# Weight splits moved to the front of the planner's order, and part of the state-space tables moved from GpSimd to VectorE and ScalarE

## The chip, the cores and the metric

The kernel runs on one core of a Trainium2 chip. The metric is the device time of one launch in microseconds (us); the median of the runs is what is compared. The profile comes from an execution of its own, and times in it are counted from the first instruction. PE is TensorE, DVE is VectorE, ACT is ScalarE, POOL is GpSimd, SP is the engine whose queue issues most of the transfers.

## The reference, cut to what matters

Two layers work on a residual stream x of 256 tokens by 2048 features, all in float32.

```
layer 0: h = rmsnorm(x);  [q k v u z_a z_b] = h @ w_in        # 2048 -> 6144
         o_a = chunked_attention(q, k, v) * silu(z_a)          # 16 heads x 64
         y   = gelu(s5(u));  o_b = y * sigmoid(y @ w_glu + b) * silu(z_b)
         x   = x + [o_a o_b] @ w_out
layer 1: h = rmsnorm(x);  [q k v z f] = h @ w_in               # forgetting attention, 16 heads x 128
         x   = x + (attention * silu(z)) @ w_out
out    = rmsnorm(x)
```

`s5` is a state-space model: for each of 64 groups of 16 channels, a state of 64 complex numbers follows x_t = A x_(t-1) + B u_t, with y_t = Re(C x_t) + D u_t. A, B and C are computed from small parameters; this is where the tables of this kernel come from.

## The kernel before, in words

**The weight stream.** Every large product is cut into column tiles of 512. For each, `project` (L135) walks over the K dimension in chunks of two 128-row blocks; `next_w` (L116) fetches a chunk (128 x 1024 float32, 512 KB) through SP's queue into `wr` (four buffers) and splits it into a rounded high part `wh` (L131, on ACT) and the rest `wl` (L132, on DVE), three buffers each. PE then does, for both blocks and both token tiles, three matmuls (high by high, L142; low weight, L143; low activation, L144), so 12 matmuls per chunk. A chunk's `wh` buffer comes free when PE has done its last matmul. There are 292 such whole chunks: a few in front for `u`, then z_b (first half), z_a, q, k, v in halves, z_b (second half), the GLU, the output projection `oe`, the 16 projections of layer 1 (`cq`, `ck`, `cv`, `cz` for four groups of heads) and its output projection `oo`.

**The state-space model.** It is done in blocks of 8 time steps. After the first half of `u` is projected, DVE computes powers of A for all groups (`pr`, `pi`, `psg`, L254 to L312). `tables(e)` then runs for e = 0..7, eight slots of groups each. It loads `bc`, and makes on DVE `bb`, `bw` (six instructions of 128 x 128, L331 to L336) and `w1` (three of 128 x 1024, L350 to L352). On POOL it makes `cc` (two of 128 x 128, L337 and L338) and `mx` (three of 128 x 1152, L357 to L359). `w1` is transposed on PE (`pm`, L366) into `min`; `mx` is stored to memory (`m_d`, L360) and multiplied with `bb` on PE (`pk`, L374) into kernels `ks`, stored as `k_d`. With the transposed input `uT`, PE forms `pv` (L408), DVE and ACT copy it (`vs`, L411 to L413), PE transposes it (`pvt`, L417) and ACT writes `X` (L419). When all eight are in, DVE runs a serial scan over the blocks: 30 steps of four instructions of 128 x 128 (L428 to L431). `s5_final` (L498) reads `k_d` and `m_d` back (L503, L508), multiplies on PE (`py`, L514 and L518), applies gelu (L520) and transposes into `yTh`, `yTl` (L536, L537), the input of the GLU product `acc_glu`.

**What can go on without the scan.** The projections z_b, z_a, q, k, v of layer 0 need only the normalised input. The GLU product needs `yTh` and `yTl`.

**What sets the order.** Tile's planner (`schedule_with_timeline_sim=True`) simulates the program and gives every engine a fixed order: among the instructions that are ready at a simulated moment, the one written earliest goes first. On the chip each engine then executes its own list strictly in that order, with semaphores between engines. `tables(0)` to `tables(2)` are written ahead of the second `u` tile, the others ahead of the gates, so table work and the scan are ahead, in priority, of the splits for z_b, z_a, q, k and v. The transfers of the weights keep their place on SP's queue.

Of the kernel before, what the change touches and what calls it, by code (L numbers as in the profile page):

```python
# [9 lines left out]
F32 = mybir.dt.float32  # L10
F32R = mybir.dt.float32r
AF = mybir.ActivationFunctionType
ALU = mybir.AluOpType
# [4 lines left out]
P = 128  # L18
L = 256
D = 2048  # L20
NT = 512
CK = 2
# [13 lines left out]
LN2_2 = math.log(2.0) - LN2_1  # L36
MAGIC = 12582912.0
PI_F = 3.1415925


@with_exitstack
def trunk(ctx: ExitStack, tc: tile.TileContext, a, out: bass.AP):
# [22 lines left out]
    nc.gpsimd.memset(mhalf, -0.5)  # L65

    def rstd_of(parts, name, n=2):
        """(sum of parts / D + EPS) ** -0.5 for n token tiles"""
        ms, r, c = (const.tile([P, n], F32, name=f"{w}_{name}") for w in ("ms", "rs", "rc"))
        nc.vector.tensor_reduce(ms, parts, axis=AX.X, op=ALU.add)  # L70
        nc.vector.tensor_scalar(ms, ms, 1.0 / D, EPS, op0=ALU.mult, op1=ALU.add)
        nc.gpsimd.tensor_tensor(r, ms, mhalf[:, 0:n], op=ALU.pow)
        nc.vector.tensor_tensor(c, r, r, op=ALU.mult)
        nc.vector.tensor_tensor(c, c, ms, op=ALU.mult)
        nc.vector.tensor_scalar(c, c, -0.5, 1.5, op0=ALU.mult, op1=ALU.add)
        nc.vector.tensor_tensor(r, r, c, op=ALU.mult)
        return r

    def vexp(pool, dst, src, n, key):
        """dst = exp(src) on [P, n], to float32's accuracy: 2^k times a polynomial"""  # L80
        V = nc.vector
        xc, kf, r, p_ = (pool.tile([P, n], F32, name=f"ve{i}_{key}", tag=f"ve{i}", bufs=1) for i in range(4))
        ki = pool.tile([P, n], mybir.dt.int32, name=f"vei_{key}", tag="vei", bufs=1)
        V.tensor_scalar(xc, src, 89.0, -90.0, op0=ALU.min, op1=ALU.max)
        V.tensor_scalar(kf, xc, 1.0 / math.log(2.0), MAGIC, op0=ALU.mult, op1=ALU.add)
        V.tensor_scalar(kf, kf, MAGIC, -127.0, op0=ALU.subtract, op1=ALU.max)
        V.scalar_tensor_tensor(r, kf, -LN2_1, xc, op0=ALU.mult, op1=ALU.add)
        V.scalar_tensor_tensor(r, kf, -LN2_2, r, op0=ALU.mult, op1=ALU.add)
        V.tensor_scalar(kf, kf, 127.0, None, op0=ALU.add)
        V.tensor_copy(ki, kf)  # L90
        V.tensor_scalar(ki, ki, 23, None, op0=ALU.logical_shift_left)
        V.tensor_scalar(p_, r, 1.0 / 5040.0, None, op0=ALU.mult)
        for c in (1.0 / 720.0, 1.0 / 120.0, 1.0 / 24.0, 1.0 / 6.0, 0.5, 1.0):
            V.scalar_tensor_tensor(p_, p_, c, r, op0=ALU.add, op1=ALU.mult)
        V.scalar_tensor_tensor(dst, p_, 1.0, ki.bitcast(F32), op0=ALU.add, op1=ALU.mult)

    def split_T(src, c, g, dh, dl, name):
        """transpose 4 K-blocks (columns c*512..) of both token tiles, scaled by g,
        into the feature-major hi/lo pair"""
        for half in range(2):  # L100
            pt = ps_tr.tile([P, 2, L], F32, name=f"pt_{name}_{c}_{half}", tag="tr")
            for kk in range(2):
                kb = c * 4 + half * 2 + kk
                for t in range(2):
                    nc.tensor.transpose(pt[:, kk, t * P:(t + 1) * P],
                                        src[:, t, kb * P:(kb + 1) * P], ident)
            for kk in range(2):
                kb = c * 4 + half * 2 + kk
                nc.scalar.activation(dh[:, kb, :], pt[:, kk, :], AF.Copy, scale=g[:, kb:kb + 1])
                nc.vector.scalar_tensor_tensor(dl[:, kb, :], pt[:, kk, :], g[:, kb:kb + 1],  # L110
                                               dh[:, kb, :].bitcast(F32), op0=ALU.mult, op1=ALU.subtract)

# [1 line left out]
    wpos = [0]  # L114

    def next_w(split=None, dst=None):  # L116
        i = wpos[0]
        wpos[0] += 1
        raw = wp.tile([P, CK * NT], F32, name=f"wr_{i}", tag="wr", bufs=4)
        if dst:  # L120
            wh, wl = dst
        else:
            wh = wp.tile([P, CK * NT], F32R, name=f"wh_{i}", tag="wh", bufs=3)
            wl = wp.tile([P, CK * NT], F32R, name=f"wl_{i}", tag="wl", bufs=3)
        step = NT if split else CK * NT
        for o in range(0, CK * NT, step):
            c = slice(o, o + step)
            nc.sync.dma_start(raw[:, c], a["w"][i][:, c])
            if split:
                split(o // NT)  # L130
            nc.scalar.activation(wh[:, c], raw[:, c], AF.Copy)  # L131
            nc.vector.tensor_tensor(wl[:, c], raw[:, c], wh[:, c].bitcast(F32), op=ALU.subtract)  # L132
        return wh, wl

    def project(ah, al, nkb, name, ready=None, by_token=False):  # L135
        """one 512-column tile of the next product for both token tiles"""
        acc = [ps_acc.tile([P, NT], F32, name=f"acc_{name}_{t}", tag="acc") for t in range(2)]

        def block(kb, wh, wl, t):
            c = slice(kb % CK * NT, (kb % CK + 1) * NT)  # L140
            sh, sl = ah[:, kb, t * P:(t + 1) * P], al[:, kb, t * P:(t + 1) * P]
            nc.tensor.matmul(acc[t], sh, wh[:, c], start=kb == 0, stop=False)  # L142
            nc.tensor.matmul(acc[t], sh, wl[:, c], start=False, stop=False)  # L143
            nc.tensor.matmul(acc[t], sl, wh[:, c], start=False, stop=kb == nkb - 1)  # L144

        if by_token:
            for t in range(2):
                for kb in range(nkb):
                    block(kb, *ready[kb // CK], t)
        else:  # L150
            for kc in range(nkb // CK):
                wh, wl = ready[kc] if ready else next_w()
                for kb in range(kc * CK, (kc + 1) * CK):
                    for t in range(2):
                        block(kb, wh, wl, t)
        return acc

    # ================= layer 0 =================
    xTh = actp.tile([P, 16, L], F32R, name="xTh", tag="ah")
    xTl = actp.tile([P, 16, L], F32R, name="xTl", tag="al")  # L160
    l0 = ctx.enter_context(ExitStack())
# [39 lines left out]
    k_d = dram.tile([NGQ, P, 2 * TC * GC], F32, name="k_d")  # L201
    m_d = dram.tile([8, P, 8, TC * GC], F32, name="m_d")

    # u columns
    uts = []
    for n in range(2):
        if n == 1:
# [16 lines left out]
                nc.scalar.activation(ut, acc[t], AF.Copy, scale=r0[:, t:t + 1])  # L224
                nc.sync.dma_start(u_d[t * P:(t + 1) * P, NT:], ut)
        if n == 0:
# [1 line left out]
            def sm(name):  # L228
                return s5.tile([P, G], F32, name=name, tag="sm_" + name)

# [84 lines left out]
            def tables(e):  # L315
# [18 lines left out]
                V.tensor_tensor(bw, bc[:, :, 1, :], gb(cr), op=ALU.mult)  # L334
                V.tensor_tensor(tt, bc[:, :, 0, :], gb(ncs), op=ALU.mult)
                V.tensor_tensor(bw, bw, tt, op=ALU.add)  # L336
                W.tensor_scalar(cc[:, 0], bc[:, :, 2, :], nsgn, None, op0=ALU.mult)  # L337
                W.tensor_scalar(cc[:, 1], bc[:, :, 3, :], -1.0, None, op0=ALU.mult)  # L338

                def pw(t_, sl):  # L340
                    n_ = len(range(9)[sl])
# [12 lines left out]
                mx = s5.tile([P, 8, 9, GC], F32, name=f"mx_{e}", tag="mx", bufs=2)  # L354
                tm = s5.tile([P, 8, 9, GC], F32, name=f"tm_{e}", tag="tm", bufs=1)
                fwd = slice(0, 9)
                W.tensor_tensor(mx, pw(pr, fwd), cc[:, 0].unsqueeze(2).to_broadcast([P, 8, 9, GC]), op=ALU.mult)  # L357
                W.tensor_tensor(tm, pw(pi, fwd), cc[:, 1].unsqueeze(2).to_broadcast([P, 8, 9, GC]), op=ALU.mult)
                W.tensor_tensor(mx, mx, tm, op=ALU.add)  # L359
                nc.sync.dma_start(m_d[e], mx[:, :, 1:9, :].rearrange("p s l c -> p s (l c)"))  # L360

                mi_ = s5b.tile([P, 8, P], F32, name=f"min_{e}", tag="min", bufs=4)
# [68 lines left out]
        V.tensor_tensor(X[:, :, :, n + 1], st1, st2, op=ALU.add)  # L431


    # gates
    zb = l0p.tile([P, 2, 2 * NT], F32, name="zb")
    zaT = l0p.tile([P, 8, L], F32, name="zaT")
    def gate(z_, nm, n):
# [16 lines left out]
    yTh = at.tile([P, 8, L], F32R, name="yTh", bufs=1)  # L454
    yTl = at.tile([P, 8, L], F32R, name="yTl", bufs=1)
    def scores(qT, kT, rows, keys):
        """causal score blocks of the heads that lie in the given rows, one row tile beside the other"""
        pscs = [ps_sc.tile([P, 3, P], F32, name=f"psc_{key}", tag="sc") for key in keys]
        for psc, r in zip(pscs, rows):
            nc.tensor.matmul(psc[:, 0, :], qT[r, 0:P], kT[r, 0:P], start=True, stop=True)  # L460
# [2 lines left out]
        return pscs  # L463

    def probs(pool, psc, bias0, bias1, key, scaled=False):
        """softmax numerators of one head, transposed per key block, and 1/sum"""
        lg = pool.tile([P, 3, P], F32, name=f"lg_{key}", tag="lg")
        mx_ = pool.tile([P, 2], F32, name=f"mx_{key}", tag="mxs", bufs=3)
        nc.vector.tensor_tensor_reduce(lg[:, 0, :], psc[:, 0, :], bias0, 1.0, LOWEST,
# [18 lines left out]
        return pT, rs  # L488

    def out_T(o_, w, dh, dl, kb, key):  # L490
        """o_ [P, 2, 128] token-major -> hi/lo K-block"""
        po = ps_tr.tile([P, L], F32, name=f"po_{key}", tag="tr")
        for t in range(2):
            nc.tensor.transpose(po[:, t * P:(t + 1) * P], o_[:, t, :], ident)
# [99 lines left out]

    gate(zb, "zb", 1)

    # GLU
    for n in range(2):
        c = slice(n * NT, (n + 1) * NT)
        y = catx.tile([P, 2, NT], F32, name=f"y_{n}")  # L600
# [25 lines left out]
        split_T(x, n, gO, x1Th, x1Tl, "x1")  # L626
    l0.close()

    # ================= layer 1 =================
    l1 = ctx.enter_context(tc.tile_pool(name="l1", bufs=2))  # L630
    r1 = rstd_of(ssp1, "1")
    r1q = const.tile([P, 2], F32, name="r1q")
# [2 lines left out]
    oTl = l1.tile([P, 16, L], F32R, name="oTl", bufs=1)  # L635

    def forget():
        # forget gates
        tri = l1.tile([P, 3 * P], F32, name="tri", bufs=1)
        nc.gpsimd.memset(tri[:, 0:P], 0.0)  # L640
        nc.gpsimd.memset(tri[:, P:3 * P], 1.0)
# [121 lines left out]
    for n in range(3):  # L763
        acc = project(oTh, oTl, 16, f"oo{n}")
        for t in range(2):
            xs = add_tile(n, acc, t)
            nc.gpsimd.tensor_tensor(xs, xs, gF[:, n * NT:(n + 1) * NT], op=ALU.mult)
    # the last tile goes one token tile after the other, its weights held on chip
    lh = actp.tile([P, 4, CK * NT], F32R, name="lh", tag="ah")
    ll = actp.tile([P, 4, CK * NT], F32R, name="ll", tag="al")  # L770
    lx = [l1.tile([P, CK * NT], F32R, name=f"lx{i}", tag="cqk") for i in range(2)]
# [13 lines left out]
            nc.sync.dma_start(ov[:, t, c * NT:(c + 1) * NT], xs)  # L785


# [1 line left out]
def _lay(inputs):  # L789
    import numpy as np  # L790

    f = {k: np.asarray(v) for k, v in inputs.items()}

    def tiles(w, n0, n1):
        """[K, N] -> chunks [(n1-n0) * K/(CK*128), 128, CK*512] of the column tiles n0..n1"""
        w = w[:, n0 * NT:n1 * NT]
        K, N = w.shape
        w = w.reshape(K // (CK * P), CK, P, N // NT, NT).transpose(3, 0, 2, 1, 4)
# [64 lines left out]
```

## Time and profile before

| what | value |
|---|---|
| runs (us) | 997.0, 997.74, 1001.69; median 997.74 |
| profiled execution, span of its instructions | 995.2 us; the page lists no other time for that execution |
| busy: PE, DVE, ACT, POOL | 946.9, 626.4, 495.7, 184.6 us |
| transfers | 191.47 MB, mean 192 GB/s |
| PE's share of the chain that ended last | 74%; DVE 15% |

The span is the time from the first to the last instruction, and the median of the runs is 2.5 us above it. A row of the page's groups gives a line, an engine, output and inputs with their shapes, a count, the busy time and the mean of one instruction in ns, and last how long the engine had been idle before these instructions and who released it. PEclk is the clock that TensorE was granted, 1.00 being full speed. Neighbouring instructions of an engine overlap by about 0.1 us in the records.

### The profile page before, as it was taken

The page shows a single profiled execution, that of the slowest core. Times are in us where ns is not written, and L with a number is a line of the kernel's source. Part 1 is how long each engine was busy: PE and PEld are TensorE (multiplying, and loading weights), DVE is VectorE, ACT ScalarE, POOL GpSimd, SP SyncE. Part 2 cuts the span into 40 slices and gives each one's busy share as a digit, 9 for nine tenths or more (in the row PEclk, how much of TensorE's full clock was granted, in tenths as well). Part 3 has the DMA queues.
Part 4 walks back from the last instruction along what each step waited for, and adds up shares of the span by engine and source line. Part 5 has one row for each costly group of instructions (what it writes and reads, how often), then busy time and mean ns, then how long its engine had stood idle before and what let it go on. Part 6 is the DMA issues. An engine that isn't in the chain of part 4 may idle for free.

```text
span 995.2 us, 13310 instructions
## 1 busy us (share of the span) xinstructions
PE 946.9 (95%) x4828; PEld 762.9 (77%) x4828; DVE 626.4 (63%) x1071; ACT 495.7 (50%) x717; POOL 184.6 (19%) x182
## 2 busy tenths in 40 slices
PE   7968788999999999999999999999999999999996
PEld 5856566887776777788888888888888888888874
DVE  7899999499962467855555445444544554455464
ACT  6623444454463367654444555445645554555451
POOL 2297974100003011000000321011001100100210
PEclk9987999999999999999999999999999999999998
DMA  8774655875569965566664654555455545554652
GB/s 303 281 218 147 189 165 175 241 214 178 163 204 263 266 207 179 167 200 204 204 225 149 212 195 153 190 182 191 155 191 184 170 153 191 185 170 155 194 196 90
DMA packets 72577, 191.47 MB, mean 192 GB/s; under 512 B 7488, under 2 KB 27184, under 8 KB 72128
## 3 DMA queue, kind: packets, MB, share of 16 engines
q1 hardware_dynamic: 71520, 188.93, 59.5%
q0 software_dynamic: 992, 1.69, 0.9%
q8 instruction: 38, 0.62, 0.3%
q14 instruction: 27, 0.22, 0.1%
HBM read 180.09 MB, written 10.50 MB: 192 GB/s over the span
## 4 chain that ended last, share of the span: by engine, by line
PE 74%; DVE 15%; DMA 4%; issue 4%; SPq 1%; ACT 1%; POOL 0%; POOLq 0%; DVEq 0%; ACTq 0%
DVE wl L132 5%; PE acc_oe L143 3%; PE acc_oe L142 3%; PE acc_oe L144 3%; PE acc_cv L142 3%; PE acc_cq L143 3%; PE acc_cq L144 3%; PE acc_cq L142 3%; PE acc_ck L142 3%; PE acc_cv L144 3%; PE acc_cv L143 3%; PE acc_cz L143 3%; PE acc_cz L144 3%; PE acc_cz L142 3%; PE acc_ck L144 3%
## 5 line engine op out<-in xcount | busy, mean ns | idle before, releaser
L132 DVE TENSOR_TENSOR wl<-wr,wh 128x1024 fp32r<-128x1024 f32 (+1 forms) x292 | 372.9, 1280 | 281.5 <-ACT wh L131 278.6
L131 ACT ACTIVATE wh<-wr 128x1024 fp32r<-128x1024 f32 (+1 forms) x292 | 307.6, 1056 | 338.8 <-PE acc_ck L144 41.8
L722 POOL TENSOR_SCALAR cbt<-ckb,cum 128x128 f32<-128x128 f32 x16 | 17.8, 1111 | 323.7 <-DVE mx_c L471 265.4
L143 PE MATMUL acc_cv<-wl,x1Th 128*128 128x512 f32 x128 | 51.1, 399 | 0.0
L143 PE MATMUL acc_oe<-wl,cTh 128*128 128x512 f32 x128 | 51.0, 399 | 0.0
L143 PE MATMUL acc_cq<-wl,x1Th 128*128 128x512 f32 x128 | 50.8, 397 | 0.0
L143 PE MATMUL acc_cz<-wl,x1Th 128*128 128x512 f32 x128 | 50.6, 395 | 0.0
L144 PE MATMUL acc_cq<-wh,x1Tl 128*128 128x512 f32 x128 | 50.5, 395 | 0.0
L144 PE MATMUL acc_oe<-wh,cTl 128*128 128x512 f32 x128 | 50.5, 395 | 0.0
L144 PE MATMUL acc_cv<-wh,x1Tl 128*128 128x512 f32 x128 | 50.3, 393 | 0.0
L144 PE MATMUL acc_cz<-wh,x1Tl 128*128 128x512 f32 x128 | 50.2, 392 | 0.0
L143 PE MATMUL acc_ck<-wl,x1Th 128*128 128x512 f32 x128 | 49.9, 390 | 0.0
L144 PE MATMUL acc_ck<-wh,x1Tl 128*128 128x512 f32 x128 | 49.9, 390 | 0.0
L142 PE MATMUL acc_cq<-wh,x1Th 128*128 128x512 f32 x128 | 48.7, 400 | 0.0
L142 PE MATMUL acc_cz<-wh,x1Th 128*128 128x512 f32 x128 | 47.6, 400 | 0.0
L142 PE MATMUL acc_oe<-wh,cTh 128*128 128x512 f32 x128 | 47.6, 399 | 0.0
L142 PE MATMUL acc_cv<-wh,x1Th 128*128 128x512 f32 x128 | 47.3, 398 | 0.0
L142 PE MATMUL acc_ck<-wh,x1Th 128*128 128x512 f32 x128 | 46.5, 392 | 0.0
L143 PE MATMUL acc_oo<-wl,oTh 128*128 128x512 f32 x108 | 42.5, 393 | 0.5 <-DVE wl L132 0.5
L144 PE MATMUL acc_oo<-wh,oTl 128*128 128x512 f32 x108 | 42.2, 391 | 0.0
L142 PE MATMUL acc_oo<-wh,oTh 128*128 128x512 f32 x108 | 39.7, 394 | 0.0
L143 PE MATMUL acc_zb<-wl,xTh 128*128 128x512 f32 x64 | 28.3, 442 | 9.4 <-DVE wl L132 9.4
(391 smaller groups left out, 2137.9 us busy)
## 6 DMA issues: line engine op xcount, KB each, us to landing
wr<-in_w_dram SPq DMA_DIRECT2D x295, 512.0 KB, 3.5
m_d<-mx SPq DMA_DIRECT2D x8, 512.0 KB, 4.9
mo<-m_d SPq DMA_DIRECT2D x8, 512.0 KB, 7.5
T<-k_d SPq DMA_DIRECT2D x40, 64.0 KB, 6.7
bc<-in_s5bc_dram SPq DMA_DIRECT2D x8, 256.0 KB, 3.3
xt<-in_x_dram SPq DMA_DIRECT2D x2, 1024.0 KB, 8.2
k_d<-ks SPq DMA_DIRECT2D x8, 256.0 KB, 3.4
bt<-in_rbx_dram SPq DMA_DIRECT2D x8, 256.0 KB, 3.7
```

The costliest lines, as they stand in the source:

```text
L131: nc.scalar.activation(wh[:, c], raw[:, c], AF.Copy)
L132: nc.vector.tensor_tensor(wl[:, c], raw[:, c], wh[:, c].bitcast(F32), op=ALU.subtract)
L142: nc.tensor.matmul(acc[t], sh, wh[:, c], start=kb == 0, stop=False)
L143: nc.tensor.matmul(acc[t], sh, wl[:, c], start=False, stop=False)
L144: nc.tensor.matmul(acc[t], sl, wh[:, c], start=False, stop=kb == nkb - 1)
L722: W.tensor_scalar(bt[:, 0, :], ckb[:, hh, 0:P], cum[:, 0, h:h + 1], None, op0=ALU.add)
```

## The change

Two edits. In `next_w` the two split instructions are traced inside a block that lets the planner treat them as though they had been written 3000 instructions earlier; the fetch stays as it was. In `tables(e)` the two `cc` instructions go from POOL to ACT, and the three `mx`/`tm` instructions go from POOL to DVE; what POOL keeps there are two memsets. Comments and docstrings are dropped too. Two extra lines move the numbering: L131, L132 become L133, L134, and so on.

```diff
+SPLIT_AHEAD = 3000
...
             if split:
                 split(o // NT)
-            nc.scalar.activation(wh[:, c], raw[:, c], AF.Copy)
-            nc.vector.tensor_tensor(wl[:, c], raw[:, c], wh[:, c].bitcast(F32), op=ALU.subtract)
+            with tc.high_priority(offset=SPLIT_AHEAD):
+                nc.scalar.activation(wh[:, c], raw[:, c], AF.Copy)
+                nc.vector.tensor_tensor(wl[:, c], raw[:, c], wh[:, c].bitcast(F32), op=ALU.subtract)
...
-                W.tensor_scalar(cc[:, 0], bc[:, :, 2, :], nsgn, None, op0=ALU.mult)
-                W.tensor_scalar(cc[:, 1], bc[:, :, 3, :], -1.0, None, op0=ALU.mult)
+                nc.scalar.activation(cc[:, 0], bc[:, :, 2, :], AF.Copy, scale=nsgn)
+                nc.scalar.activation(cc[:, 1], bc[:, :, 3, :], AF.Copy, scale=-1.0)
...
-                W.tensor_tensor(mx, pw(pr, fwd), cc[:, 0].unsqueeze(2).to_broadcast([P, 8, 9, GC]), op=ALU.mult)
-                W.tensor_tensor(tm, pw(pi, fwd), cc[:, 1].unsqueeze(2).to_broadcast([P, 8, 9, GC]), op=ALU.mult)
-                W.tensor_tensor(mx, mx, tm, op=ALU.add)
+                V.tensor_tensor(mx, pw(pr, fwd), cc[:, 0].unsqueeze(2).to_broadcast([P, 8, 9, GC]), op=ALU.mult)
+                V.tensor_tensor(tm, pw(pi, fwd), cc[:, 1].unsqueeze(2).to_broadcast([P, 8, 9, GC]), op=ALU.mult)
+                V.tensor_tensor(mx, mx, tm, op=ALU.add)
```

## The prediction, made before the changed kernel was run

> **What bounds the kernel now.** I read the busy times by stage first, with stretches cut where the work changes: the tables (50 to 180 us), the scan (200 to 275), the end of the state-space model (296 to 350), then layer 0's rest and layer 1.
>
> ```profile
> core 0: us, PE busy (x) PEld busy (x) DVE busy (x) ACT busy (x) POOL busy (x), PEclk, DMA share, GB/s
> 0.00:50.00 50.00, 42.93 (x176) 34.58 (x177) 39.78 (x129) 32.54 (x45) 13.43 (x23) 1.00 0.82 292
> 50.00:180.00 130.00, 104.81 (x615) 80.11 (x614) 125.47 (x125) 52.30 (x81) 96.62 (x48) 0.89 0.60 183
> 180.00:200.00 20.00, 20.00 (x135) 16.00 (x134) 8.34 (x11) 9.44 (x14) 3.97 (x9) 1.00 0.87 230
> 200.00:275.00 75.00, 72.21 (x341) 57.37 (x340) 73.33 (x180) 37.62 (x57) 0.53 (x2) 1.00 0.60 187
> 296.00:350.00 54.00, 50.77 (x451) 37.26 (x451) 20.03 (x25) 20.25 (x28) 9.60 (x19) 0.97 1.02 262
> 420.00:950.00 530.00, 530.00 (x2506) 438.28 (x2505) 270.97 (x414) 270.25 (x366) 49.13 (x72) 1.00 0.56 184
> 950.00:995.20 45.20, 35.13 (x153) 28.15 (x151) 22.70 (x33) 14.71 (x21) 5.08 (x4) 0.92 0.42 140
> ```
>
> PE bounds nearly everything: from 420 to 950 us it is busy all the time at full clock, so nothing there can be won. The place that is open is 50 to 180: PE works 104.81 of 130 us at clock 0.89, while DVE is busy 125.47. At full clock its work is 104.81 x 0.89 = 93.3 us, so 130 - 93.3 = **36.7 us** are lost there: 25.2 idle, 11.5 by the clock. The 7 us before the first matmuls and the 10 us at the end are untouched by the edits. Next, what PE waits for in that stretch, and what one such wait looks like in order of time:
>
> ```profile
> PE acc_za L143 <- DVE wl L132: 9.6, 5, 4.1
> PE acc_zb L143 <- DVE wl L132: 9.4, 4, 5.7
> PE pm L366 <- DVE w L352: 3.7, 2, 2.2
> PE pvt L417 <- DVE vs L413: 1.4, 1, 1.4
> PE pv L408 <- DVE ks L380: 1.1, 1, 1.1
> ```
> ```profile
> 70.71 3.71 POOL L359 TENSOR_TENSOR mx<-mx,tm 128x1152 f32<-128x1152 f32 x1
> 71.84 3.66 DVE L352 TENSOR_TENSOR w<-w,tw 128x1024 f32<-128x1024 f32 x1
> 72.31 0.40 PE L144 MATMUL acc_zb<-wh,xTl 128*128 128x512 f32 x1
> 72.54 0.40 PE L143 MATMUL acc_zb<-wl,xTh 128*128 128x512 f32 x1
> 75.56 1.28 PE L366 MATMUL pm<-ident,w 128*128 128x128 f32 x8 [2.16 <-DVE w L352]
> 77.06 0.63 PE L144 MATMUL acc_zb<-wh,xTl 128*128 128x512 f32 x1
> 77.48 0.63 PE L142 MATMUL acc_zb<-wh,xTh 128*128 128x512 f32 x1
> ```
>
> 19.0 of the 25.2 idle us wait for `wl`, always DVE; 6.2 wait for results of the tables. And DVE is slow for a reason: its `w` starts at 71.84, POOL's `mx` ends at 74.42, and `w` ends at 75.50, 1.1 us after that. It stood still until POOL was done. After the wait, matmuls start 0.42 us apart (77.06, 77.48) where just before it was 0.23 (72.31, 72.54).
>
> **What leaves POOL, and what its instructions cost DVE.** The groups of POOL and DVE, those of DVE in the table stretch, the last two DVE rows and the split in the scan stretch serving as its undisturbed price:
>
> ```profile
> L359 POOL TENSOR_TENSOR mx<-mx,tm 128x1152 f32<-128x1152 f32 x8 | 27.1, 3385 | 0.4
> L357 POOL TENSOR_TENSOR mx<-pr,cc 128x1152 f32<-128x1152 f32 x8 | 25.2, 3154 | 7.0 <-DVE rs L76 4.6 <-DMA m_d<-mx 2.4
> L358 POOL TENSOR_TENSOR tm<-pi,cc 128x1152 f32<-128x1152 f32 x8 | 21.4, 2675 | 0.7 <-DVE pi L287 0.7
> L337 POOL TENSOR_SCALAR cc<-bc,nsgn 128x128 f32<-128x128 f32 x8 | 16.1, 2015 | 20.8 <-DVE ve_dt L88 16.5 <-DMA bc<-in_s5bc_dram 4.3
> L327 POOL MEMSET bb<- 128x256 f32 x8 | 2.6, 325 | 4.8 <-PE pk L374 4.8
> ```
> ```profile
> L132 DVE TENSOR_TENSOR wl<-wr,wh 128x1024 fp32r<-128x1024 f32 x27 | 47.7, 1778 | 0.9 <-ACT wh L131 0.9
> L352 DVE TENSOR_TENSOR w<-w,tw 128x1024 f32<-128x1024 f32 x8 | 18.1, 2260 | 0.1
> L351 DVE TENSOR_TENSOR tw<-psg,bw 128x1024 f32<-128x1024 f32 x8 | 10.0, 1247 | 0.1
> L333 DVE TENSOR_TENSOR bb<-bb,tt 128x128 f32<-128x128 f32 x8 | 9.0, 1130 | 0.0
> L336 DVE TENSOR_TENSOR bw<-bw,tt 128x128 f32<-128x128 f32 x8 | 6.8, 846 | 0.1
> L334 DVE TENSOR_TENSOR bw<-bc,cr 128x128 f32<-128x128 f32 x6 | 5.8, 962 | 0.6 <-DMA bc<-in_s5bc_dram 0.6
> L332 DVE TENSOR_TENSOR tt<-bc,cs 128x128 f32<-128x128 f32 x8 | 2.5, 316 | 0.0
> ```
> ```profile
> L132 DVE TENSOR_TENSOR wl<-wr,wh 128x1024 fp32r<-128x1024 f32 x24 | 29.2, 1222 | 1.5 <-ACT wh L131 1.5
> L431 DVE TENSOR_TENSOR X<-st,st 128x128 f32<-128x128 f32 x30 | 12.1, 402 | 0.8
> ```
>
> The same split takes 1.778 us here and 1.222 in the scan, where POOL is busy 0.53 of 75 us. The excess: splits 27 x 0.556 = 15.0; `w` 8 x (2.260 - 1.222) = 8.3; against the 0.316 of L332, L333 8 x 0.814 = 6.5, L336 8 x 0.530 = 4.2, L334 6 x 0.646 = 3.9. That is 37.9 us of DVE time that is waiting, not work. All of it goes with POOL's operations, since only memsets of about 0.3 us stay.
>
> The Trainium skill says the same in SBUF — State Buffer, "Who interferes with whom": a VectorE instruction with two SBUF inputs and a GpSimd instruction that reads SBUF exclude each other for the whole instruction, while GpSimd writing alone does not. By that rule the memsets left on POOL cost nothing and every two-input row above may be held. The `w` row that ends 1.1 us after `mx` agrees.
>
> **What DVE gains in work.** 24 instructions of 128 x 1152. No row shows them on DVE; the nearest is L351, which reads the same power table in the same broadcast form: 1.247 for 1024, so 1.40 for 1152, 24 x 1.40 = **33.7 us**. From below, the split's 1.222 as it stands gives 29; from above, POOL's own prices give 27.1 + 25.2 + 21.4 = 73.7. I take 33.7, since L351 is of the same engine and form. DVE in the stretch then needs 125.5 - 37.9 + 33.7 = 121.3 (about 117 to 161 by the ends): almost no relief of its load by itself. The gain must come from the order.
>
> **What ACT gains.** 16 copies of 128 x 128 with a scale. The nearest is a larger copy:
>
> ```profile
> L411 ACT COPY vs<-pv 128x256 f32<-128x256 f32 x8 | 3.0, 373 | 3.2 <-PE pv L408 3.2
> ```
>
> At most 16 x 0.373 = 6 us, against 77 us in which ACT is idle from 50 to 180; from below, nothing. On the path of a table it replaces POOL's 2.0 us. It is taken as nothing; without that cover it is 6.
>
> **The order.** A split is now taken as soon as its chunk and its buffer are there, ahead of tables, scan and attention. One chunk feeds PE for 12 x 0.23 = 2.7 us and asks 1.2 of DVE and about as much of ACT. So PE can be fed always, and DVE's other half is left to the tables. What is pushed back: `bb`, `w`, `mx`, and behind them `pm`, `pk`, `pv`, the scan, `s5_final`. Let the tables be done T after 50. DVE's share without splits is 121.3 - 27 x 1.222 = 88; the splits take 1.222 / 2.73 = 0.45 of the time PE gives to chunks. Of PE's 93.3, 324 chunk matmuls at 0.23 make 74, so 19 go to small ones. T = 88 + 0.45 (T - 19), T = 144: the tables end at 194 rather than 180. In these 144 us PE does 144 of work where it now does 93 + 14 = 107 (the 14 from the busy row 180 to 200). So PE is the full **36.7 us** further, and the tables are 14 late. Who waits for them:
>
> ```profile
> L431 DVE TENSOR_TENSOR X<-st,st x30: 386/403/417, 202.5 to 271.0; 128x128 f32<-128x128 f32 x30
> L518 PE MATMUL py<-mo,X x128: 272/273/421, 296.2 to 337.0; 128*32 128x128 f32 x128
> L537 DVE TENSOR_TENSOR yTl<-pyt,yTh x4: 680/686/692, 344.0 to 350.1; 128x512 fp32r<-128x512 f32 x4
> L142 PE MATMUL acc_glu<-wh,yTh x32: 388/389/499, 376.4 to 404.4; 128*128 128x512 f32 x32
> ```
>
> The scan ends at 271.4, `py` starts 25 us later although nothing more is computed for it, `yTl` is done at 350.8 and the GLU starts at 376. Slack of 25 and 25, 50 together. Needed are 14 (later tables) + 36.7 (PE arriving earlier) = 51. So the slack is just eaten up: I charge 3 us.
>
> **What stays lost.** The scan stretch shows what DVE at 73.33 of 75 leaves idle on PE without POOL: 2.8 us. Over 130 us that is 4.8. Of the 6.2 us for table results, which the splits' rank doesn't cure, half was POOL's holding; 3 stay. Together 8 (from 0 to 15 with some slow clock behind each gap).
>
> **Sum.** 995.2 - 36.7 + 8 + 3 = 969.5 for the span; the median of the runs lies 997.74 - 995.2 = 2.5 above it: **972 us**.
>
> **Rivals.**
>
> 1. *The tables become the bound* (20%). If the moved instructions cost 1.75 us rather than 1.40, DVE has 8.4 more, the tables end 8.4 / 0.55 = 15 later, and the GLU waits for that beyond the 3 charged: 972 + 12 = 984. At about 2.05 us each the gain would be gone. For it: slack is used up to a microsecond. Against: L351.
> 2. *No clock loss, nothing late* (10%). All gaps that stay are short, so the clock holds at 1.00, and the 2.8 us of the scan stretch close too: 995.2 - 36.7 - 2.8 + 5 + 2.5 = 963. For it: 1.00 in the scan stretch, whose gaps are short. Against: 77.06, slow after gaps of no more than 2.16 us. TensorE: Matmul & The Clock Gate, "What's actually happening", in the Trainium skill has the clock fall after an idle window of about 3.4 us; by that rule this result would be likelier, and the row after 2.16 us doesn't agree.
> 3. *The rank does nothing* (10%): splits wait for buffers that PE frees, not for their turn. Then DVE's 121.3 for 125.5 stays, and the gain is 4 plus half of the clock loss: 995.2 - 10 + 2.5 = 988. Against: 5.7 us of wait in one piece, longer than any buffer turn of 2.7.
> 4. *Slower: a split at the head of DVE's queue stands waiting for `wh`, and tables and scan stand behind it* (9%). The work to the scan's end is 88 + 4 x 30 x 0.40 = 136 us of DVE. With w us of standing per chunk its share is 1 - (1.222 + w) / 2.73. After the scan 55 us follow at least (296 to 351, first `py` to last `yTl`). For a GLU start at 376, as now, the scan must end at 321, in 271 us: share 0.502, w = 0.14. Past that point the change loses; at w = 0.25 the share is 0.46, the scan ends at 345, the GLU starts at 400: 24 us late, 995.2 + 24 + 2.5 = 1022. For it: in-order queues, and w enters each of 80 chunks. Against: the scan row shows 1.5 us of such idle for 24 splits, 0.06 each.
>
> The forecast has 51%, its own range 962 to 982. A difference of 0.5% (5 us) is about what a measurement of this kernel can tell from none. Under 992.7 lie the forecast and rivals 1, 2 and 3, less a twentieth for the upper part of 1 and 3: faster 0.85, same 0.06, slower 0.09. The range takes in rival 2 and most of 1 and 3: 957 to 990.
>
> **What would show it.** Right: split and table rows of DVE at 1.22 and 0.3 in the table stretch, the moved rows near 1.4, POOL nearly idle there, PE over 95% busy at clock 0.97 or more, PE's waits for `wl` under 5 us. The step on slack: the GLU starting near 340 with no wait of PE between the scan's end and it; a wait for `py` or `yTh` there of over 10 us is rival 1. Wrong: DVE idle before splits in the table stretch (rival 4), moved rows at 2 us or more, or table rows still held with POOL idle. Layer 1 should be as long as before; a gap there would be something that I haven't seen.

## The result and the profile after

The changed kernel takes 974.81 us (971.64 to 975.55, median of four) against 997.39 us before: a ratio of 0.9762, interval 0.9736 to 0.9787. The forecast was 972. The time was met; the experiments below show that the edit on which most of the gain was put, the rank of the splits, brought none of it.

Busy time by stretch of the changed kernel, the columns as in the prediction:

```profile
50.00:180.00 130.00, 124.33 (x791) 98.88 (x790) 115.05 (x163) 67.27 (x110) 7.68 (x21) 0.97 0.77 241
180.00:200.00 20.00, 20.00 (x100) 16.54 (x98) 18.48 (x41) 11.54 (x16) 0.00 (x0) 1.00 0.62 175
200.00:275.00 75.00, 70.93 (x384) 53.48 (x383) 66.22 (x177) 37.14 (x66) 1.32 (x5) 1.00 0.54 172
275.00:296.00 21.00, 17.83 (x138) 13.67 (x136) 7.35 (x6) 8.29 (x10) 5.78 (x12) 0.99 1.06 246
296.00:350.00 54.00, 52.13 (x343) 39.39 (x344) 25.77 (x45) 23.10 (x38) 5.74 (x8) 0.91 0.84 236
420.00:950.00 530.00, 530.00 (x2501) 438.17 (x2500) 275.31 (x413) 265.78 (x360) 50.65 (x74) 1.00 0.56 185
```

Counted as in the prediction (stretch less PE's busy time at the granted clock), the table stretch now loses 130 - 124.33 x 0.97 = 9.4 us where it lost 36.7: 27.3 us won. Part is given back later. The stretch 200 to 275 loses 4.1 (2.8 before), and what lies between 275 and 350 loses 3.4 + 6.6 = 10.0 (4.8 before, all of it from 296 on). In layer 1 nothing moved: 530.00 of 530.00, as before.

VectorE's groups in the table stretch, and ScalarE's two new ones:

```profile
L134 DVE TENSOR_TENSOR wl<-wr,wh 128x1024 fp32r<-128x1024 f32 x36 | 43.6, 1217 | 3.0 <-ACT wh L133 2.9
L360 DVE TENSOR_TENSOR tm<-pi,cc 128x1152 f32<-128x1152 f32 x8 | 10.8, 1349 | 0.3 <-ACT cc L340 0.3
L354 DVE TENSOR_TENSOR w<-w,tw 128x1024 f32<-128x1024 f32 x8 | 9.7, 1215 | 0.0
L335 DVE TENSOR_TENSOR bb<-bb,tt 128x128 f32<-128x128 f32 x8 | 2.2, 280 | 0.0
```
```profile
L339 ACT ACTIVATE cc<-bc,nsgn 128x128 f32<-128x128 f32 x6 | 2.4, 400 | 5.4 <-DMA bc<-in_s5bc_dram 5.4
L340 ACT ACTIVATE cc<-bc 128x128 f32<-128x128 f32 x6 | 1.8, 294 | 0.0
```

Each VectorE row that was held before is at its undisturbed price again: the split 1.217 us (1.778 before), `w` 1.215 (2.260), `bb` 0.280 (1.130). Nine more splits fit into the same 130 us, beside the work that came from GpSimd. What PE still waits for in the first 420 us, the five longest behind the start (at the start it waits 6.3 us for the first `wh`, as before):

```profile
PE py L520 <- DMA mo<-m_d: 3.3, 3, 2.1
PE acc_zb L145 <- DVE wl L134: 2.3, 1, 2.3
PE pm L368 <- DVE w L354: 1.9, 1, 1.9
PE py L516 <- DMA T<-k_d: 1.6, 1, 1.6
PE acc_q L145 <- DVE wl L134: 1.6, 3, 0.7
```

The waits of `acc_za` and `acc_zb` for a split, 19.0 us between 50 and 180 us before, are 2.3 now. The longest in total, behind the start, is now for the read-back of `m_d`. The state-space chain, the store of the tables before and after, then scan, `yTl` and GLU after:

```profile
L360 SPq DMA_DIRECT2D m_d<-mx x8: 524/525/608, 68.8 to 170.6; - x8
```
```profile
L362 SPq DMA_DIRECT2D m_d<-mx x8: 524/525/597, 66.7 to 161.0; - x8
L433 DVE TENSOR_TENSOR X<-st,st x30: 377/398/414, 182.2 to 253.6; 128x128 f32<-128x128 f32 x30
L539 DVE TENSOR_TENSOR yTl<-pyt,yTh x4: 680/686/692, 324.0 to 329.9; 128x512 fp32r<-128x512 f32 x4
L144 PE MATMUL acc_glu<-wh,yTh x32: 389/389/500, 353.4 to 381.0; 128*128 128x512 f32 x32
```

The last table is stored 10 us earlier, the scan ends 17 us earlier (254.0 for 271.4), and the GLU starts 23 us earlier (353.4 for 376.4). The whole gain is there by that point, and the tables didn't fall behind for it: VectorE's last `w` ends at 170.9 us, where it ended at 172.5.

### The profile page after: what moved, and what is told of

It reads as the page before. It is cut to its first block, busy times and chain, and to the rows that moved or that the text cites. A ratio compares the mean times of both kernels' runs of the same rounds, so it can differ in the third digit from the quotient of the medians.

```text
span 973.5 us, 13313 instructions
## 1 busy us (share of the span) xinstructions
PE 941.0 (97%) x4828; PEld 758.7 (78%) x4828; DVE 603.9 (62%) x1095; ACT 494.4 (51%) x730; POOL 84.5 (9%) x142
## 4 chain that ended last, share of the span: by engine, by line
PE 79%; DVE 11%; DMA 5%; issue 3%; ACT 1%; SPq 0%; POOL 0%; POOLq 0%; DVEq 0%; ACTq 0%
DVE wl L134 4%; PE acc_oe L145 3%; PE acc_oe L144 3%; PE acc_oe L146 3%; PE acc_cv L144 3%; PE acc_cq L145 3%; PE acc_cq L146 3%; PE acc_cq L144 3%; PE acc_ck L144 3%; PE acc_cv L145 3%; PE acc_cz L145 3%; PE acc_cz L146 3%; PE acc_cz L144 3%; PE acc_cv L146 3%; PE acc_ck L145 3%; PE acc_ck L146 3%
## 5 line engine op out<-in xcount | busy, mean ns | idle before, releaser
L134 DVE TENSOR_TENSOR wl<-wr,wh 128x1024 fp32r<-128x1024 f32 (+1 forms) x292 | 357.3, 1226 | 286.1 <-ACT wh L133 282.4
L133 ACT ACTIVATE wh<-wr 128x1024 fp32r<-128x1024 f32 (+1 forms) x292 | 307.6, 1056 | 302.8 <-PE acc_ck L146 41.8
L724 POOL TENSOR_SCALAR cbt<-ckb,cum 128x128 f32<-128x128 f32 x16 | 10.3, 642 | 328.8 <-DVE mx_c L473 271.0
L144 PE MATMUL acc_u<-wh,xTh 128*128 128x512 f32 x64 | 23.8, 412 | 6.3 <-ACT wh L133 6.3
```

The source lines that it names most:

```text
L724: W.tensor_scalar(bt[:, 0, :], ckb[:, hh, 0:P], cum[:, 0, h:h + 1], None, op0=ALU.add)
```

## The experiments

All are timed against the kernel before; the changed kernel's ratio for comparison is 0.9762.

**1. The rank of the splits alone.** The kernel before with the two split instructions inside the block that ranks them ahead.

```diff
-            nc.scalar.activation(wh[:, c], raw[:, c], AF.Copy)
-            nc.vector.tensor_tensor(wl[:, c], raw[:, c], wh[:, c].bitcast(F32), op=ALU.subtract)
+            with tc.high_priority(offset=SPLIT_AHEAD):
+                nc.scalar.activation(wh[:, c], raw[:, c], AF.Copy)
+                nc.vector.tensor_tensor(wl[:, c], raw[:, c], wh[:, c].bitcast(F32), op=ALU.subtract)
```

> The kernel before with the splits ranked ahead alone; cc, mx and tm stay on GpSimd. Theory A (each edit does its own part: the rank takes PE's waits for wl away, the move takes away the holding of VectorE by GpSimd): VectorE stays held, its splits at 1.7 us and w at 2.2 us in the table stretch, PE's waits for wl fall from 19 us to under 8, the tables end later than in the kernel before, and the time is 980 to 986, about half of the gain. Rival B (the rank does everything): 975. Rival C (the rank does nothing, the move everything): 995 or more.

Measured: 1003.64 us, ratio 1.0055 (1.0040 to 1.0070). Slower by half a per cent. The table stretch, VectorE's groups in it, and PE's waits over the run:

```profile
50.00:180.00 130.00, 99.96 (x610) 76.67 (x609) 123.14 (x125) 51.17 (x80) 98.68 (x48) 0.93 0.59 180
```
```profile
L134 DVE TENSOR_TENSOR wl<-wr,wh 128x1024 fp32r<-128x1024 f32 x27 | 45.6, 1697 | 0.9 <-ACT wh L133 0.9
L354 DVE TENSOR_TENSOR w<-w,tw 128x1024 f32<-128x1024 f32 x8 | 14.2, 1778 | 0.1
```
```profile
PE acc_zb L145 <- DVE wl L134: 13.8, 6, 5.7
PE acc_za L145 <- DVE wl L134: 9.6, 6, 2.9
```

The same 27 splits in the stretch, still held, and PE waits 23.4 us for them, not the 8 of theory A. VectorE's list says why. For each split I counted how many other instructions stand ahead of it in the order in which VectorE executed them. Of the 27 splits in the table stretch, 24 didn't move against the kernel before, and the other three moved by three places at most; over the whole kernel, 182 of 292 didn't move. So the rank left the planned order of that stretch as it was; why the planner made no more of it isn't shown. Theory A falls in its half about the rank, and so does B; C comes nearest, though not even it had the kernel get slower. Why it is 5 us slower is open. PE loses 130 - 99.96 x 0.93 = 37.0 us in the table stretch, as before. In the profiled executions, which are 7 us apart, the splits run 1 us later at 274 us and 7 us later at 430, and between the two the rank does move splits, by up to 18 places.

**2. The move alone.** The changed kernel without that block.

```diff
-            with tc.high_priority(offset=SPLIT_AHEAD):
-                nc.scalar.activation(wh[:, c], raw[:, c], AF.Copy)
-                nc.vector.tensor_tensor(wl[:, c], raw[:, c], wh[:, c].bitcast(F32), op=ALU.subtract)
+            nc.scalar.activation(wh[:, c], raw[:, c], AF.Copy)
+            nc.vector.tensor_tensor(wl[:, c], raw[:, c], wh[:, c].bitcast(F32), op=ALU.subtract)
```

> The changed kernel with the splits back at their written rank; only the move of cc to ScalarE and of mx and tm to VectorE stays. Theory A: splits at 1.22 us, w at 1.22 us, VectorE's table work ends earlier than in the kernel before by 10 us or more, PE still waits for wl behind runs of table instructions (5 to 12 us), time 982 to 988. Rival B: 995. Rival C: 975.

Measured: 974.51 us, ratio 0.9766 (0.9750 to 0.9782): the changed kernel's time. Its stretch and its splits there:

```profile
50.00:180.00 130.00, 125.56 (x804) 100.20 (x803) 115.05 (x166) 69.22 (x115) 7.68 (x21) 0.97 0.78 240
```
```profile
L133 DVE TENSOR_TENSOR wl<-wr,wh 128x1024 fp32r<-128x1024 f32 x35 | 42.7, 1226 | 2.2 <-ACT wh L132 2.2
```

So the move is the change, and the rank adds nothing to it: rival C of both expectations. But the move does two things. It takes GpSimd's reading work away from beside VectorE, and it makes the planner give VectorE another list: 52 splits stand ahead of the last `w` of the tables here and in the changed kernel, where it was 40 before (40 in run 1 too). The splits did go ahead of the tables, through the move and not through the rank. I formed a narrower theory from this: what counts is VectorE's time lost while GpSimd holds it. To measure it, take every VectorE instruction from 50 to 180 us beyond the median of its form in the changed kernel: 52 us are held in the kernel before, 50 in run 1, 1 here.

**3 and 4. GpSimd busy again, reading or only writing.** In the first, nine extra multiplications per table call read `pr`, `pi`, `psg` and `cc`; in the second, 22 extra memsets stand behind the memset of `bb`. Both write a tile that nobody reads.

```diff
# 3, behind the three lines of mx and tm
+                dm = s5.tile([P, 8, 3, GC], F32, name=f"dm_{e}", tag="dm", bufs=1)
+                for i in range(9):
+                    l3 = slice(i // 3 * 3, i // 3 * 3 + 3)
+                    W.tensor_tensor(dm, pw((pr, pi, psg)[i % 3], l3),
+                                    cc[:, i % 2].unsqueeze(2).to_broadcast([P, 8, 3, GC]), op=ALU.mult)
...
# 4, behind the memset of bb
+                dm = s5.tile([P, 8, 3, GC], F32, name=f"dm_{e}", tag="dm", bufs=1)
+                for _ in range(22):
+                    tc.keep_in_program_order(W.memset(dm, 0.0))
```

> The changed kernel with nine extra GpSimd multiplications of 128x384 per table call, 72 in all, which read pr, pi, psg and cc and write a tile that nobody reads; work is only added, and it computes nothing new. Theory A (a GpSimd instruction that reads SBUF holds VectorE instructions with two inputs): the split's mean in the table stretch rises from 1.22 us to 1.4 or more, w from 1.22 to 1.5 or more, time 978 to 988. Rival D (VectorE was slow for another cause, its load or the order): split and w stay at 1.22, time 975 within 2.

> The changed kernel with 22 extra GpSimd memsets of 128x384 per table call, 176 in all, into a tile that nobody reads; work is only added. Theory A with reading as the condition: split and w stay within 3% of 1.22 us, time 975 within 3. Rival E (any busy GpSimd holds VectorE): split and w rise as in the run with the reading instructions.

Measured: with reads 1019.41 us, ratio 1.0213 (1.0198 to 1.0228); with memsets 975.99 us, ratio 0.9775 (0.9739 to 0.9812). Of the run with memsets, the split and the added instructions in the table stretch:

```profile
L134 DVE TENSOR_TENSOR wl<-wr,wh 128x1024 fp32r<-128x1024 f32 x36 | 43.8, 1223 | 2.6 <-ACT wh L133 2.5
```
```profile
L332 POOL MEMSET dm<- 128x384 f32 x132 | 55.4, 419 | 6.9
```

55 us of GpSimd time that only writes leave the split at 1.223 us and the time where it was, so rival E falls. The Trainium skill gives this condition in SBUF — State Buffer, "Who interferes with whom": a VectorE instruction with two SBUF inputs contends with a GpSimd instruction that reads SBUF, not with one that only writes it. This run agrees. In the reading run the split rose to 1.457 us and `w` to 1.626, as theory A had it, so rival D falls. But it cost 45 us, far more than expected, and its test is not clean: the memset of `bb` stands in GpSimd's queue too, and VectorE waited for it.

```profile
DVE bb L333 <- POOL bb L329: 10.3, 3, 7.7
```

**5. Reads where the memsets stood.** Six multiplications of 128x384 per call, placed like the memsets of run 4, on `pr`, `pi` and `psg`, which all but the first of them find finished.

```diff
+                dm = s5.tile([P, 8, 3, GC], F32, name=f"dm_{e}", tag="dm", bufs=1)
+                for i in range(6):
+                    l3 = slice(i // 2 * 3, i // 2 * 3 + 3)
+                    ps_ = (pr if i % 2 else psg)[:, l3, s0:s0 + 8].rearrange("p l s -> p s l").unsqueeze(3)
+                    pb_ = pi[:, l3, s0:s0 + 8].rearrange("p l s -> p s l").unsqueeze(3)
+                    tc.keep_in_program_order(
+                        W.tensor_tensor(dm, ps_.to_broadcast([P, 8, 3, GC]), pb_.to_broadcast([P, 8, 3, GC]), op=ALU.mult))
```

> The changed kernel with six extra GpSimd multiplications of 128x384 per table call, 48 in all, placed behind the memset of bb exactly where the run with the extra memsets has its 22, reading the finished tables pr, pi and psg only, so that no table waits for a GpSimd result that it did not wait for there; work is only added. Theory A (reading holds VectorE): split and w above 1.4 us in the table stretch and a time of 985 to 1005, against the 976 of the memsets of about the same GpSimd time. Rival F (the 45 us of the earlier run with reading instructions came from the tables waiting in GpSimd's queue, not from holding): split and w near 1.22, time 974 to 980.

Measured: 1004.99 us, ratio 1.0065 (1.0043 to 1.0087). The split in the table stretch, then a wait of VectorE from 50 to 210 us:

```profile
L134 DVE TENSOR_TENSOR wl<-wr,wh 128x1024 fp32r<-128x1024 f32 x32 | 42.9, 1348 | 0.4 <-ACT wh L133 0.4
```
```profile
DVE bb L340 <- POOL bb L329: 8.9, 2, 6.6
```

The time is what theory A named and `w` is at 1.549 us, the split is held less than it named (1.348, not over 1.4), and 8.9 us of queue are in it again: GpSimd's reads took longer than the memsets they replaced (96 us for 55 in the stretch), and the first waited 14.4 us for `psg`, so the memset of `bb` came late. Both theories have a part here; the place of the splits in VectorE's list has none, since every split has as many other instructions ahead of it as in run 4. Runs 9 and 10 take the queue out.

**6 and 7. Which of the moved instructions matters.** In 6 only `mx` and `tm` move and `cc` stays on GpSimd; in 7 only `cc` moves. The splits keep their written rank in both.

```diff
# 6, against the kernel before: the three lines of mx and tm, of which the last is shown
...
-                W.tensor_tensor(mx, mx, tm, op=ALU.add)
+                V.tensor_tensor(mx, mx, tm, op=ALU.add)
...
# 7, against the kernel before: the two lines of cc, of which the last is shown
...
-                W.tensor_scalar(cc[:, 1], bc[:, :, 3, :], -1.0, None, op0=ALU.mult)
+                nc.scalar.activation(cc[:, 1], bc[:, :, 3, :], AF.Copy, scale=-1.0)
```

> The kernel before with only the three 128x1152 instructions moved to VectorE; cc stays on GpSimd, the splits at their written rank. Theory A: what holds is GpSimd time that reads, and 16 small cc instructions are a quarter of it in the kernel before, so some holding stays: split mean 1.25 to 1.35 in the table stretch, time 976 to 984. Rival G (cc does not matter): 974.5 within 2.

> The kernel before with only the two cc copies moved to ScalarE; mx and tm stay on GpSimd. Theory A: three quarters of the holding stays: split mean 1.5 to 1.75, PE waits 15 us or more for wl, time 988 to 997. Rival H (the small cc instructions were the ones that did the harm, since each breaks in between two VectorE instructions): below 984.

Measured: 6 takes 973.58 us, ratio 0.9766 (0.9731 to 0.9801), the whole gain; 7 takes 997.20 us, ratio 0.9992 (0.9977 to 1.0007), nothing. Of run 6, the split in the table stretch and GpSimd's `cc`, then one `cc` and VectorE's first free moment in order of time:

```profile
L133 DVE TENSOR_TENSOR wl<-wr,wh 128x1024 fp32r<-128x1024 f32 x36 | 43.7, 1222 | 0.6 <-ACT wh L132 0.6
```
```profile
L339 POOL TENSOR_SCALAR cc<-bc 128x128 f32<-128x128 f32 x6 | 13.5, 2257 | 0.0
```
```profile
63.86 9.03 POOL L339 TENSOR_SCALAR cc<-bc 128x128 f32<-128x128 f32 x1
...
72.84 0.31 POOL L328 MEMSET bb<- 128x256 f32 x1
```
```profile
72.66 1.23 DVE L133 TENSOR_TENSOR wl<-wr,wh 128x1024 fp32r<-128x1024 f32 x1 [0.15 <-ACT wh L132]
```

With `cc` alone on GpSimd, VectorE isn't held at all (the split at 1.222; 0.5 us over the whole stretch). It is GpSimd that stands: one `cc` lasts 9.03 us and ends at 72.89, just after VectorE has been idle for 0.15 us. The other eleven of the stretch last 0.52 to 2.93 us, and some end without such a gap, so what lets GpSimd go on isn't shown. Theory A of run 6 expected holding in proportion to GpSimd's reading time; that falls, and rival G was right. Of run 7, groups of the table stretch and one wait:

```profile
L132 DVE TENSOR_TENSOR wl<-wr,wh 128x1024 fp32r<-128x1024 f32 x28 | 33.7, 1216 | 2.4 <-ACT wh L131 2.4
L333 DVE TENSOR_TENSOR bb<-bb,tt 128x128 f32<-128x128 f32 x8 | 14.0, 1751 | 0.0
```
```profile
PE acc_za L143 <- DVE wl L132: 12.6, 3, 7.8
```

Here the holding fell on other instructions: `bb` at 1.751 and not one split is held, yet PE waits 12.6 us for splits of z_a, in three pieces, and 9.3 us for those of z_b. A split that is itself at full speed stands behind held instructions in the same queue: ahead of the wait of 7.8 us VectorE ran a `w` of 3.27 us (1.21 in the changed kernel) and a `bw` of 2.70 (0.28). The held time of the stretch is 52 us as in the kernel before, though a fifth of GpSimd's reading time is gone, which fits a gain of nothing. Theory A expected a quarter of the holding to go: the time is 0.2 us above its upper end, PE's waits are over its 15 us, and the place of the holding is another. Rival H falls.

**8. Less work on VectorE.** The kernel of run 2 without `tm` and the sum that follows. This leaves out the second half of the output tables.

```diff
...
-                V.tensor_tensor(tm, pw(pi, fwd), cc[:, 1].unsqueeze(2).to_broadcast([P, 8, 9, GC]), op=ALU.mult)
-                V.tensor_tensor(mx, mx, tm, op=ALU.add)
```

> The changed kernel, splits at their written rank, without the tm instruction and the sum that follows, so mx holds only the first product and the tables of the outputs are incomplete; 16 VectorE instructions of 1.35 us, 21.6 us of VectorE time, are gone. Theory A (once held time is gone VectorE has room, and PE is the bound with the residue of the read-back stage): 966 to 973, at most a third of the 21.6 us. Rival I (VectorE's load still sets the end): 953 to 960.

Measured: 970.50 us, ratio 0.9721 (0.9691 to 0.9752). 21.6 us of VectorE's work bring about 4 us, and the interval touches that of run 2. Its stretch, and the split there with the idle time ahead of it:

```profile
50.00:180.00 130.00, 126.87 (x827) 101.70 (x826) 102.80 (x163) 72.90 (x120) 7.93 (x21) 1.00 0.81 248
```
```profile
L133 DVE TENSOR_TENSOR wl<-wr,wh 128x1024 fp32r<-128x1024 f32 x37 | 45.0, 1220 | 21.2 <-ACT wh L132 21.2
```

VectorE now has 21.2 us of idle time in which it waits for the next chunk, for ScalarE's `wh`, which in turn waits mostly for a buffer that PE frees: PE sets the pace. So two thirds of the 32 us that came over from GpSimd cost only about 4 us where they are, and rival I falls.

**9 and 10. Holding alone, with its control.** The memsets of `bb` and `ks` go to VectorE, so nothing of the tables is in GpSimd's queue. Run 9 adds four multiplications per call that read the finished `w1`; run 10 doesn't.

```diff
-                W.memset(bb, 0.0)
+                V.memset(bb, 0.0)
...
+                dm = s5.tile([P, 8, 3, GC], F32, name=f"dm_{e}", tag="dm", bufs=1)
+                for i in range(4):
+                    W.tensor_tensor(dm, w1[:, :, i:i + 3, :], w1[:, :, i + 1:i + 4, :], op=ALU.mult)
...
-                nc.gpsimd.memset(ks[:, :, 0:P], 0.0)
+                V.memset(ks[:, :, 0:P], 0.0)
```

> The changed kernel with the memsets of bb and ks done on VectorE, so that no table waits for anything in GpSimd's queue, and four extra GpSimd multiplications of 128x384 per table call, 32 in all, that read the finished w1 and write a tile that nobody reads; work is only added. Theory A (holding alone costs time): w and the split above 1.3 us in the table stretch, VectorE busy over 122 of its 130 us for no more chunks, time 980 to 992. Rival F (what cost time in the two earlier runs with reading instructions was the wait of the tables in GpSimd's queue): within 2 us of the control run without the extra instructions.

> The control: the changed kernel with the memsets of bb and ks done on VectorE and no extra instructions. Both theories: 974 to 978, VectorE some 16 times 0.3 us busier.

Measured: 9 takes 991.56 us, ratio 0.9937 (0.9920 to 0.9953); the control 976.14 us, ratio 0.9783 (0.9766 to 0.9799). Run 9, groups of the table stretch, and a piece in order of time:

```profile
L134 DVE TENSOR_TENSOR wl<-wr,wh 128x1024 fp32r<-128x1024 f32 x35 | 46.4, 1329 | 0.0
L364 DVE TENSOR_TENSOR mx<-mx,tm 128x1152 f32<-128x1152 f32 x8 | 13.2, 1649 | 0.0
```
```profile
90.47 7.34 POOL L357 TENSOR_TENSOR dm<-w 128x384 f32<-128x384 f32 x4 [11.97 <-DVE w L354]
```
```profile
90.66 2.02 DVE L134 TENSOR_TENSOR wl<-wr,wh 128x1024 fp32r<-128x1024 f32 x1
92.61 1.10 DVE L333 TENSOR_TENSOR bb<-bc,cr 128x128 f32<-128x128 f32 x1
```

The control, the same two groups:

```profile
L134 DVE TENSOR_TENSOR wl<-wr,wh 128x1024 fp32r<-128x1024 f32 x36 | 43.4, 1209 | 2.0 <-ACT wh L133 1.7
L361 DVE TENSOR_TENSOR mx<-mx,tm 128x1152 f32<-128x1152 f32 x8 | 10.8, 1347 | 0.0
```

32 GpSimd instructions whose results nobody needs cost 15.4 us. VectorE is never idle in the stretch in run 9, a split takes 0.12 us more and an `mx` 0.30 more, and no VectorE instruction there waits for a GpSimd result. F falls. Theory A holds, with one limit: VectorE's lists in the two runs are the same for 317 instructions, up to 185 us in the control, and by the last of these run 9 is 10.4 us behind. After that the planner gave run 9 another order, in which 22 splits have up to 19 more of the other instructions ahead of them. So about 10 of the 15 us are shown to come from holding alone; what the new order has of the rest isn't shown.

The runs with added reads agree on the size. Held time is counted here from 50 to 210 us, less that of the run it is compared with; all but the last column are of the profiled executions.

| compared | VectorE held (us) | VectorE waits for `bb` in GpSimd's queue (us) | time lost (us) |
|---|---|---|---|
| 9 against 10 | 19 | 0 | 15.4 |
| 5 against 4 | 22 | 8.9 | 29.0 |
| 3 against the changed kernel | 35 | 10.3 | 44.6 |

For the change itself the same sum is 52 us of holding less 32 us of work that came over: 20 us, beside a gain of 22.6. That leaves little for the new list, but no run has the time freed with VectorE's old list, so the share of the order isn't shown.

No run beats the changed kernel beyond its interval while computing everything. Run 6 has the same time with three changed lines.

## Why the prediction was right, point by point

**What bounds, and where.** Right: PE's loss lay between 50 and 180 us, and 27.3 of the 36.7 us came back there. Layer 1 and both ends stayed.

**VectorE held by GpSimd.** Right, and shown by runs 9 and 10 as far as their lists are the same, and by run 5 against run 4 together with a queue. The size was too small. The term had 37.9 us from the rows it used. These rows of the kernel before, in the same stretch, were left out of it:

```profile
L350 DVE TENSOR_TENSOR w<-pr,bb 128x1024 f32<-128x1024 f32 x8 | 11.9, 1486 | 0.0
L331 DVE TENSOR_TENSOR bb<-bc,cr 128x128 f32<-128x128 f32 x6 | 5.8, 967 | 0.0
L215 DVE TENSOR_SCALAR ut<-ut,rs 128x512 f32<-128x512 f32 x2 | 3.0, 1477 | 0.0
L289 DVE TENSOR_SCALAR psg<-pi,sgn 128x576 f32<-128x576 f32 x1 | 2.9, 2898 | 0.0
L196 DVE TENSOR_SCALAR r0q<-rs 128x2 f32<-128x2 f32 x1 | 2.2, 2246 | 0.0
```

Taking every group of that stretch against the same group after the change gives about 52 us: L350 is 2.2 of it, L331 4.1, the last three about 6.5, and the small groups that were counted are at 0.28 rather than 0.316. The last three aren't instructions with two input tiles: they multiply one tile by a scalar. They were held all the same (`psg` 2.898 us for 0.515), and in run 7 so was a plain copy, `e<-psg`, at 2.27 us where the changed kernel has 0.18. The prediction looked at rows with two inputs alone.

**What the move costs.** Right: 1.35 us each where 1.40 was taken, 32.3 us for 33.7; on ACT 0.400 and 0.294 each, hidden.

**The order.** Wrong, and this is the step that failed: "almost no relief of its load by itself. The gain must come from the order." With 37.9 us of holding against 33.7 of new work, the relief seemed to be 4 us. It is 52 - 32 = 20: VectorE needs 115.05 - 9 x 1.217 = 104 us for the 27 splits of before, not 121. And the rank, which was to bring the order, brought nothing (runs 1 and 2); the list in which 52 splits stand ahead of the last `w`, for 40 before, came with the move. Rival 3 had the right outcome for the rank with the wrong price of 988, from the same small term; its reason, that splits wait for buffers, isn't shown. The row held against it, a wait of 5.7 us in one piece, longer than a buffer's turn, didn't speak for rank: run 1 has the same 5.7 with the splits ranked ahead. In the kernel before VectorE ran an `ut` of 2.48 us ahead of that split, and the split itself took 3.28: it was a queue of held instructions, as in run 7.

**The tables late, the slack just used.** Wrong, from the same term: T was worked out with 88 us of other VectorE work, and it was 115.05 - 43.6 = 71.5. With that, T = 71.5 + 0.45 (T - 19) gives 114, the tables' end at 164. The last `w` ends at 170.9 and the last store is issued at 161.0, so the tables came earlier, not 14 us later. The GLU started at 353, not near 340, and PE waited 4.9 us ahead of it, where no wait was expected.

**What stays lost.** 8 us were named for the table stretch, it is 9.4. The 3 us charged for late tables weren't lost to tables. Between 275 and 350 us PE loses 5.2 us more than before: its waits for the read-back of `T` and `mo` there are 4.9 us (2.9 before), and its clock from 296 to 350 is 0.91 (0.97 before). The two errors, about 16 us too little relief and a whole step of credit to the rank, offset each other, so that 972 came close to 974.8 is in part luck.

**Rivals 1, 2 and 4.** Not seen. The moved instructions kept to 1.35 us; the clock in the table stretch rose to 0.97, not 1.00; VectorE stood 2.9 us in all before 36 splits, 0.08 each.

## What to carry to other kernels

When VectorE's rows of one form differ in mean between stretches, and GpSimd is busy in the slow one with two-input elementwise work, take the difference over every group of the stretch as VectorE time that a move gives back, the small groups too, before looking at the order. Compare the engine's lists before and after an edit: a rank can leave them as they were, and a move of work to another engine can change them without being asked to. Where an instruction is waited for, look at what it has ahead of it in its queue, and whether that is held. Work that comes over to VectorE is cheap as long as it still idles for its chunks; beyond that point being held is paid for in the kernel's time (15 us for 32 small instructions, of which some 10 are shown to be holding).

## What the runs showed of the hardware that I had not expected

GpSimd isn't always the holder. Its two-input multiplications held VectorE (split 1.329 us in run 9, 1.778 in the kernel before), but its one-input `cc` in run 6 left VectorE's split at 1.222 and stood itself, once for 9.03 us, while ten two-input instructions of VectorE ran one behind the other. The instructions differ in size too (128x128 for `cc`, 128x384 and 128x1152 for the others), so that the number of inputs makes the difference isn't shown. The Trainium skill says in SBUF — State Buffer, "Who interferes with whom", that the order of issue decides who blocks, and not the shape of the instruction. No run here separates the two; by the row of 9.03 us, the engine that is blocked can wait for more than one instruction of the other.

Being held isn't limited to VectorE instructions with two input tiles either: a copy of 128x64 took 2.27 us in run 7 beside GpSimd's `tm`, and 0.18 in the changed kernel.

```profile
66.30 3.35 POOL L358 TENSOR_TENSOR tm<-pi,cc 128x1152 f32<-128x1152 f32 x1
67.44 2.27 DVE L308 COPY e<-psg 128x64 f32<-128x64 f32 x1
```
